# One VectorE sum of each seven-product unit moved behind three low parts

## The chip, the cores and the metric

The kernel runs on one core of one Trainium2 chip. The metric is the device time of one execution in microseconds (us). TensorE does the matmuls, VectorE (DVE in the profile) and ScalarE (ACT) prepare their operands, SyncE (SP) issues the transfers of the weights, and GpSimd (POOL) does a few small operations.

## The reference, cut to what matters

Two layers act on 256 positions of width 2048, in float32. Each layer is an input projection, two groups of heads (spatial gating and dilated attention), an output projection, and a feed-forward part:

```python
def reference(x, mix_norm, w_in, ..., w_gate, w_up, w_down):
    for l in range(DEPTH):
        ...
        x = x + mixed @ w_out[l]
        h = rms_norm(x, ffn_norm[l])
        x = x + (jax.nn.silu(h @ w_gate[l]) * (h @ w_up[l])) @ w_down[l]
    return x
```

The change lies in the feed-forward part: `w_gate` and `w_up` are 2048 x 5632, `w_down` is 5632 x 2048.

## The kernel before, in words

**Three matmuls for one.** To keep float32's precision, each operand is split in two parts. The high part (`wh`) is a copy of the tile rounded to fp32r, made on ScalarE; the low part (`wl`) is the tile minus its high part, made on VectorE (`split_w`, line 832). For each 128-row step, `mm3` (line 854) issues three matmuls: high x high, high x low and low x high, so the second matmul is the first that reads the weights' low part. Line 91 in the profile is the helper through which all instructions of ScalarE and VectorE go; they are told apart by their tiles.

**A unit.** In the feed-forward part, `unit` (line 892) multiplies a 2 x 2 arrangement of activation blocks by a 2 x 2 arrangement of weight blocks with seven products in place of eight. The weight blocks are raw tiles `b11`, `b12`, `b22` and `b21`, each loaded by one transfer (128 x 2048 elements where the unit has s = 4 steps, 128 x 1024 where s = 2). Sums of them are needed:

- `early` makes `e` = b12 - b11, then b12 = b22 - b12, before the unit's first item;
- `p1` splits b11, then makes b11 = b11 + b12;
- `p5` splits `e`, `p6` splits b11, `p2` makes b11 = b21 - b11 and splits b21, `p7` splits b12, `p3` splits b22, and `p4` splits b11.

So the seven products come in the order r1, r5, r6, r2, r7, r3, r4, here called the first to the seventh. The sum for the seventh product (b21 - b11) is made in `p2`, the preparation of the fourth. The first, fourth, ... products add into four banks of PSUM: the first and fourth into bank 1 (`C` in the profile), the second into Z (`CZ`), the third, fifth and seventh into X (`CX`), the sixth into Y (`CY`). Between products ScalarE copies banks: after the first product CX<-C, after the second `s`<-CZ, after the third CY<-CX, after the fifth `s`<-CX. After the sixth and the seventh, VectorE adds the saved copies to Z and Y.

Behind its seven products a unit has four plain items, which split one raw tile each and run 24 matmuls each.

**The order of the work.** The program is unrolled, and each engine runs its instructions in the order in which they are written out. All items, of all units, stand in one list. Before item n runs, `prep_more` (line 1065) writes out the preparations that fit a ring of six slots (two a full-size item): at full size that is the preparation of item n + 2. So the preparation of the sixth product (`p3`) is written behind the third product and its copy, and that of the seventh (`p4`) behind the fourth product. In the first unit of a layer's feed-forward part the sums begin five items ahead in place of one.

**The raw tiles.** `live` counts raw tiles in use; a preparation that is done with one lowers it, and `dma_more` issues the next load while it is under five. A layer has 17 units: chunks of four gate/up units and two down units twice, then a chunk of three gate/up units and two down units of s = 2. While a unit runs, jobs of others (the transposes `hTp` of the finished hidden block, and their copies `xg`) are written out between its matmuls.

The lines that the change touches are `p2` (929) and `p4` (942).

Of the kernel before, what the change touches and what calls it, by code (L numbers as in the profile page):

```python
# [12 lines left out]
ALU = mybir.AluOpType  # L13
# [129 lines left out]
def trunk_kernel(ctx: ExitStack, tc: tile.TileContext, aps: dict):  # L143
# [21 lines left out]
    def slot(shape, dtype, name):  # L165

        return gen.tile(list(shape), dtype, tag="g", name=name)
# [61 lines left out]
    def add(steps, limit=BACKLOG_NS):  # L229
        jobs.append(Job(steps, limit))  # L230
        jobs.sort(key=lambda job: -job.limit)

    def run_jobs(extra=0):
        for job in list(jobs):
            if job.t + MARGIN_NS <= q.pe and (job.when is None or job.when()):
                if q.backlog() <= job.limit + extra:
                    job.step()

    def drain(ready):
        stuck = 0  # L240
        while not ready():
            assert stuck < 2000, "operand is never made"
            stuck += 1
            q.pe += 100
            run_jobs(1000)
# [387 lines left out]
    def form(F, f, src):  # L633
        hi, lo = F.at(f)
        act.activation(out=hi, in_=src, func=ACTF.Copy)
        dve.tensor_tensor(out=lo, in0=src, in1=hi.bitcast(F32), op=ALU.subtract)
        F.ready.add(f)
# [169 lines left out]
    live = [0]  # L807
# [4 lines left out]
    def dma_one(r):  # L812
        n = sum(src.shape[1] for src in r.srcs)
        r.tile = slot([P, n, W], F32, "raw")
        k = 0
        for src in r.srcs:
            nc.sync.dma_start(out=r.tile[:, k:k + src.shape[1], :], in_=src)
            k += src.shape[1]
        live[0] += 1
# [6 lines left out]
    def need(r):  # L826
        while r.tile is None:
            dma_one(raws[n_raw[0]])
            n_raw[0] += 1
        return r.tile  # L830

    def split_w(src, parts=1):

        n = src.shape[1]
        if 2 * n <= 4:
            both = slot([P, 2, n, W], F32R, "w")
            wh, wl = both[:, 0], both[:, 1]
        else:
            wh, wl = slot([P, n, W], F32R, "wh"), slot([P, n, W], F32R, "wl")
        saved, q.chain = q.chain, q.pe  # L840
        for k in range(parts):
            sl = slice(k * n // parts, (k + 1) * n // parts)
            act.activation(out=wh[:, sl, :], in_=src[:, sl, :], func=ACTF.Copy)
            dve.tensor_tensor(
                out=wl[:, sl, :], in0=src[:, sl, :], in1=wh[:, sl, :].bitcast(F32), op=ALU.subtract)
        q.chain = saved
        return wh, wl

    def w_sum(out, in0, in1, op):
        saved, q.chain = q.chain, q.pe  # L850
        dve.tensor_tensor(out=out, in0=in0, in1=in1, op=op)
        q.chain = saved

    def mm3(out, x, wh, wl, start, stop):
        hi, lo = x
        for n, (a, b) in enumerate(((hi, wh), (hi, wl), (lo, wh))):
            nc.tensor.matmul(  # L857
                out=out, lhsT=a, rhs=b, start=start and n == 0, stop=stop and n == 2,
                skip_group_check=True)
# [32 lines left out]
    def unit(s, quarter, plains, form, done, lead=1):  # L892

        bank = {}
        b11, b12, b22, b21 = (Raw([quarter(*kn)], UNIT_RAW) for kn in ((0, 0), (0, 1), (1, 1), (1, 0)))
        raws.extend((b11, b12, b22, b21))
        U = {}

        def new_bank(name):
            drain(lambda: mm_lease.free)
            mm_lease.free.pop(0)
            bank[name] = mm_p.tile([P, W], F32, tag="mm", name="C" + name)

        def copy(out, in_):
            saved, q.chain = q.chain, q.pe
            act.activation(out=out, in_=in_, func=ACTF.Copy)
            q.chain = saved

        def early():
            x11, x12, x22 = need(b11), need(b12), need(b22)
            U["e"] = slot([P, s, W], F32, "e")
            live[0] += 1
            w_sum(U["e"], x12, x11, ALU.subtract)
            w_sum(x12, x22, x12, ALU.subtract)

        def p1(it, parts=1):
            it.w = split_w(b11.tile)
            w_sum(b11.tile, b12.tile, b11.tile, ALU.add)  # L920

        def p5(it, parts=1):
            it.w = split_w(U["e"])
            live[0] -= 1

        def p6(it, parts=1):
            it.w = split_w(b11.tile)

        def p2(it, parts=1):
            w_sum(b11.tile, need(b21), b11.tile, ALU.subtract)  # L930
            it.w = split_w(b21.tile)
            live[0] -= 1

        def p7(it, parts=1):
            it.w = split_w(b12.tile)
            live[0] -= 1

        def p3(it, parts=1):
            it.w = split_w(b22.tile)
            live[0] -= 1  # L940

        def p4(it, parts=1):
            it.w = split_w(b11.tile)
            live[0] -= 1

        def product(it, f, name, start):
            wh, wl = it.w
            for k in range(s):
                x = form(f, k)
                mm3(bank[name], x, wh[:, k, :], wl[:, k, :], start and k == 0, k == s - 1)  # L950
                q.pe += 3 * MM_NS
                run_jobs()

        def r1(it):
            new_bank("1")
            product(it, "11", "1", True)
            new_bank("X")
            copy(bank["X"], bank["1"])

        def r5(it):  # L960
            new_bank("Z")
            product(it, "S1", "Z", True)
            U["s5"], U["s3"] = (tmp.tile([P, W], F32, tag="u", name=n) for n in ("s5", "s3"))
            copy(U["s5"], bank["Z"])

        def r6(it):
            product(it, "S2", "X", False)
            new_bank("Y")
            copy(bank["Y"], bank["X"])

        def r2(it):
            product(it, "12", "1", False)

        def r7(it):
            product(it, "S3", "X", False)
            copy(U["s3"], bank["X"])

        def r3(it):
            product(it, "S4", "Y", False)
            w_sum(bank["Z"], bank["Z"], U["s3"], ALU.add)  # L980

        def r4(it):
            product(it, "22", "X", False)
            w_sum(bank["Y"], bank["Y"], U["s5"], ALU.add)

        for p, r in ((p1, r1), (p5, r5), (p6, r6), (p2, r2), (p7, r7), (p3, r3), (p4, r4)):
            items.append(Item(1 if s <= 2 else 2, UNIT_RING, p, r))
        early_at[len(items) - 7 - lead] = early

        names = {(0, 0): "1", (1, 0): "Y", (0, 1): "X", (1, 1): "Z"}  # L990
        for i, (n, srcs, ops) in enumerate(plains):
            r = Raw(srcs, UNIT_RAW)
            raws.append(r)

            def prep(it, parts=1, r=r):
                it.w = split_w(need(r))
                live[0] -= 1

            def run(it, i=i, n=n, ops=ops):
                wh, wl = it.w  # L1000
                for t in range(NT):
                    for k, op in enumerate(ops):
                        mm3(bank[names[n, t]], op(t), wh[:, k, :], wl[:, k, :], False, k == len(ops) - 1)
                        q.pe += 3 * MM_NS
                        run_jobs()
                    if i >= len(plains) - 2:
                        add(done(n, t, bank[names[n, t]]), FFN_LIMIT)
            items.append(Item(2, UNIT_RING, prep, run))
# [238 lines left out]
```

## Time and profile before

| | |
|---|---|
| median of 3 runs | 2277.02 us (2276.92 to 2278.56) |
| profiled execution | 2275.85 us, of which the span of the trace is 2273.7 us |
| TensorE busy | 2255.7 us (99%) |
| VectorE busy | 1828.6 us (80%) |
| ScalarE busy | 1322.1 us (58%) |
| moved by DMA | 440.34 MB, 194 GB/s |

Times in rows are in microseconds from the start of the span, and the name after an arrow in brackets is what ended the idle time before an instruction. `wl<-raw,wh` is an instruction that writes tile `wl` and reads tiles `raw` and `wh`. Rows of a timeline merge instructions that follow one another directly (x2 with one start and one duration). The end of a matmul is modelled.

### The profile page before, as it was taken

The numbers are of one execution on the slowest core, as the hardware profiler recorded it, in microseconds if no ns is written. First come the engines' busy times: TensorE is split into PE (matmuls) and PEld (weight loads), VectorE is DVE, ScalarE is ACT, GpSimd is POOL, SyncE is SP. The second block draws the span as 40 slices with busy tenths as digits, with TensorE's granted clock in tenths as the row PEclk, the third lists the DMA queues.
The fourth block names the chain that finished last, engine by engine and source line by source line (L and its number), as shares of the span: only waits on it lengthen the run. The fifth ranks groups of instructions, "written<-read, shape, count | busy, mean of one in ns | idle before, by whom it ended". The sixth has DMA issues, their size and how long they took to land.

```text
span 2273.7 us, 25953 instructions
## 1 busy us (share of the span) xinstructions
PE 2255.7 (99%) x10249; PEld 1863.7 (82%) x10249; DVE 1828.6 (80%) x1721; ACT 1322.1 (58%) x1590; POOL 59.2 (3%) x36
## 2 busy tenths in 40 slices
PE   9999999999999999999999999999999999999999
PEld 6888888888788888888888888888888888888887
DVE  6666766889999889988765666768998988989886
ACT  6555664565665665656655555646566546556563
POOL 0010000000000000000000001000000000000000
PEclk9999999999999999999999999999999999999999
DMA  9554545464564554745645444555546556447453
GB/s 351 192 185 151 182 152 215 165 227 154 186 246 180 209 209 149 259 185 192 227 167 196 163 167 167 185 185 196 192 167 215 211 194 223 176 168 275 167 204 111
DMA packets 66939, 440.34 MB, mean 194 GB/s; under 512 B 8065, under 2 KB 8577, under 8 KB 16769
## 3 DMA queue, kind: packets, MB, share of 16 engines
q1 hardware_dynamic: 66816, 438.69, 53.7%
q8 instruction: 80, 1.31, 0.2%
q14 instruction: 43, 0.34, 0.0%
HBM read 436.56 MB, written 2.10 MB: 193 GB/s over the span
## 4 chain that ended last, share of the span: by engine, by line
PE 82%; DVE 10%; issue 4%; ACT 2%; DMA 1%; SPq 0%; DVEq 0%; ACTq 0%
PE Z L857 33%; PE CX L857 16%; PE C L857 12%; PE CY L857 9%; PE CZ L857 8%; DVE wl L91 6%; DVE raw L91 1%; PE sc L473 1%; ACT wh L91 1%; DVE e L91 1%; PE hTp L260 1%; DMA gn<-in_k_norm 1%; PE qkp L260 1%; PE o L505 0%; DVE s L91 0%
## 5 line engine op out<-in xcount | busy, mean ns | idle before, releaser
L91 DVE TENSOR_TENSOR wl<-raw,wh 128x2048 fp32r<-128x2048 f32 x316 | 717.0, 2286 | 124.8 <-ACT wh L91 123.9
L91 ACT ACTIVATE wh<-raw 128x2048 fp32r<-128x2048 f32 x316 | 598.1, 1913 | 165.8 <-DVE wl L91 54.9
L857 PE MATMUL Z<-w,xT 128*128 128x512 f32 x2688 | 641.0, 395 | 3.6 <-ACT w L91 1.4
L857 PEld LDWEIGHTS Z<-w,xT 128*128 128x128 f32 x2688 | 499.0, 188 | 107.9 <-ACT w L91 2.3
L91 DVE TENSOR_TENSOR w<-raw,w 128x1024 fp32r<-128x1024 f32 (+1 forms) x313 | 376.5, 1216 | 216.5 <-ACT w L91 212.3
L91 ACT ACTIVATE w<-raw 128x1024 fp32r<-128x1024 f32 (+1 forms) x313 | 315.6, 1050 | 21.9 <-DMA raw<-in_w_in 9.8
L91 DVE TENSOR_TENSOR raw<-raw 128x2048 f32<-128x2048 f32 (+1 forms) x102 | 220.6, 2163 | 2.5
L857 PE MATMUL CX<-wh,fF 128*128 128x512 f32 x528 | 175.5, 391 | 0.0
L857 PE MATMUL C<-wh,fF 128*128 128x512 f32 x352 | 117.2, 391 | 0.0
L857 PEld LDWEIGHTS CX<-wh,fF 128*128 128x128 f32 x528 | 99.1, 188 | 20.4
L857 PE MATMUL C<-wh,fT 128*128 128x512 f32 x352 | 115.5, 389 | 0.0
L857 PE MATMUL CY<-wh,fT 128*128 128x512 f32 x352 | 115.5, 389 | 0.0
L857 PE MATMUL CZ<-wh,fT 128*128 128x512 f32 x352 | 115.5, 389 | 0.0
L857 PE MATMUL CX<-wh,fT 128*128 128x512 f32 x352 | 115.5, 389 | 0.0
L857 PE MATMUL CX<-wl,fF 128*128 128x512 f32 x264 | 102.7, 389 | 0.0
L857 PE MATMUL Z<-w,bT 128*128 128x512 f32 x384 | 89.9, 391 | 0.0
L91 ACT ACTIVATE CX<-C 128x512 f32<-128x512 f32 x34 | 19.8, 582 | 120.3 <-PE C L857 120.3
L857 PE MATMUL Z<-w,aT 128*128 128x512 f32 x384 | 88.8, 390 | 0.0
L857 PEld LDWEIGHTS Z<-w,aT 128*128 128x128 f32 x384 | 71.8, 188 | 14.8
L857 PEld LDWEIGHTS Z<-w,bT 128*128 128x128 f32 x384 | 71.8, 188 | 14.7
L857 PE MATMUL CY<-wh,fF 128*128 128x512 f32 x240 | 79.9, 391 | 0.0
L857 PEld LDWEIGHTS C<-wh,fT 128*128 128x128 f32 x352 | 66.1, 188 | 13.7
(191 smaller groups left out, 3444.9 us busy)
## 6 DMA issues: line engine op xcount, KB each, us to landing
raw<-in_w_in SPq DMA_DIRECT2D x109, 1024.0 KB, 4.8
raw<-in_w_gate SPq DMA_DIRECT2D x88, 1024.0 KB, 4.9
raw<-in_w_up SPq DMA_DIRECT2D x88, 1024.0 KB, 4.9
raw<-in_w_down SPq DMA_DIRECT2D x72, 1024.0 KB, 4.8
raw<-in_w_out SPq DMA_DIRECT2D x32, 1024.0 KB, 4.8
raw<-in_w_down SPq DMA_DIRECT2D x32, 512.0 KB, 5.0
raw<-in_w_in SPq DMA_DIRECT2D x5, 512.0 KB, 8.0
xstage<-in_xT SPq DMA_DIRECT2D x8, 256.0 KB, 7.5
```

What stands on the lines that cost most here:

```text
L91: return f(**kw)
L260: nc.tensor.transpose(out=tp[:, i, t * P:(t + 1) * P], in_=src_of(t)[:, (c0 + i) * P:(c0 + i + 1) * P], identity=ident)
L473: nc.tensor.matmul(out=sc[:, g, :n], lhsT=L.kv[pair, g][:, h, t * P:(t + 1) * P], rhs=kT[:, h, :n], start=True, stop=True)
L857: nc.tensor.matmul(out=out, lhsT=a, rhs=b, start=start and n == 0, stop=stop and n == 2, skip_group_check=True)
```

## The change

The sum b11 = b21 - b11 goes from the front of `p2` to the front of `p4`. `p2` is left with the split of b21. Raw tile b21 is given back in `p4` in place of `p2`, so `live` falls by two there. The number of instructions is the same.

```diff
         def p2(it, parts=1):
-            w_sum(b11.tile, need(b21), b11.tile, ALU.subtract)
-            it.w = split_w(b21.tile)
-            live[0] -= 1
+            it.w = split_w(need(b21))
...
         def p4(it, parts=1):
+            w_sum(b11.tile, b21.tile, b11.tile, ALU.subtract)
             it.w = split_w(b11.tile)
-            live[0] -= 1
+            live[0] -= 2
```

On VectorE a unit's order of these was: sum, fourth low part, fifth, sixth, seventh. It becomes: fourth low part, fifth, sixth, sum, seventh. On ScalarE the order of the copies is as before.

## Rows read from the trace of the kernel before

**Rows 1.** The page's first part: engine, busy us, share of the span, instructions.

```profile
PE 2255.7 (99%) x10249; PEld 1863.7 (82%) x10249; DVE 1828.6 (80%) x1721; ACT 1322.1 (58%) x1590; POOL 59.2 (3%) x36
```

**Rows 2.** The tile `e` on VectorE, one instruction a unit: durations ns, first and last start.

```profile
L91 DVE TENSOR_TENSOR e<-raw x34: 1214/2283/2291, 421.7 to 2225.2; 128x2048 f32<-128x2048 f32 x30, 128x1024 f32<-128x1024 f32 x4
```

**Rows 3.** Timeline of VectorE in a gate/up unit: start, duration, instruction, count, [idle before].

```profile
1036.43 2.28 DVE L91 TENSOR_TENSOR raw<-raw 128x2048 f32<-128x2048 f32 x1
...
1041.11 2.29 DVE L91 TENSOR_TENSOR wl<-raw,wh 128x2048 fp32r<-128x2048 f32 x1 [0.20 <-ACT wh L91]
1043.83 4.49 DVE L91 TENSOR_TENSOR wl<-raw,wh 128x2048 fp32r<-128x2048 f32 x2 [0.43 <-ACT wh L91]
```

**Rows 4.** Timeline of ScalarE in the same unit.

```profile
1041.39 0.58 ACT L91 ACTIVATE CY<-CX 128x512 f32<-128x512 f32 x1 [0.31 <-PE CX L857]
1041.89 3.71 ACT L91 ACTIVATE wh<-raw 128x2048 fp32r<-128x2048 f32 x2
1045.50 0.58 ACT L91 ACTIVATE xg<-hTp 128x512 f32<-128x512 f32 x1
1047.76 0.60 ACT L91 ACTIVATE s<-CX 128x512 f32<-128x512 f32 x1 [1.68 <-PE CX L857]
1048.25 1.91 ACT L91 ACTIVATE wh<-raw 128x2048 fp32r<-128x2048 f32 x1
```

**Rows 5.** Timeline of TensorE in the same unit: transposes, seventh product, first plain item.

```profile
1044.60 1.04 PE L260 MATMUL hTp<-ident,s 128*128 128x128 f32 x8
...
1050.51 0.39 PE L857 MATMUL CX<-wl,fF 128*128 128x512 f32 x1
...
1053.23 0.39 PE L857 MATMUL C<-wl,fT 128*128 128x512 f32 x1
```

**Rows 6.** Timeline of VectorE in the fourth unit of layer 0.

```profile
576.63 2.28 DVE L91 TENSOR_TENSOR raw<-raw 128x2048 f32<-128x2048 f32 x1
578.83 8.89 DVE L91 TENSOR_TENSOR wl<-raw,wh 128x2048 fp32r<-128x2048 f32 x4
```

**Rows 7.** Timeline of TensorE in that unit, at the fourth product.

```profile
581.17 0.50 PE L857 MATMUL C<-wl,fF 128*128 128x512 f32 x1 [1.21 <-DVE wl L91]
```

**Rows 8.** The list of waits: engine, line, what for; us in total, times, longest.

```profile
PEld C L857 <- DVE wl L91: 15.9, 17, 1.7
...
ACT w L91 <- DMA raw<-in_w_in: 9.8, 5, 3.7
...
PE C L857 <- DVE wl L91: 8.5, 8, 1.3
```

**Rows 9.** The tile `hTp` on TensorE: durations ns, first and last start.

```profile
L260 PE MATMUL hTp<-ident,s x176: 270/273/273, 497.7 to 2220.7; 128*128 128x128 f32 x176
```

**Rows 10.** Timeline of VectorE in the first gate/up unit of the second chunk.

```profile
709.44 4.49 DVE L91 TENSOR_TENSOR wl<-raw,wh 128x2048 fp32r<-128x2048 f32 x2 [0.43 <-ACT wh L91]
```

**Rows 11.** Timeline of TensorE in that unit, at the seventh product.

```profile
715.19 0.39 PE L857 MATMUL CX<-wl,fF 128*128 128x512 f32 x1
```

**Rows 12.** Timeline of VectorE in the first down unit of the first chunk.

```profile
620.81 6.88 DVE L91 TENSOR_TENSOR wl<-raw,wh 128x2048 fp32r<-128x2048 f32 x3
```

**Rows 13.** Timeline of TensorE in that unit, at the seventh product.

```profile
632.37 0.39 PE L857 MATMUL CX<-wl,hF 128*128 128x512 f32 x1
```

**Rows 14.** Timeline of VectorE in a down unit of half-size tiles: the seventh low part.

```profile
1077.96 1.23 DVE L91 TENSOR_TENSOR w<-raw,w 128x1024 fp32r<-128x1024 f32 x1 [1.07 <-ACT w L91]
```

**Rows 15.** Timeline of TensorE in that unit: the seventh product's first matmuls.

```profile
1083.42 1.30 PE L857 MATMUL CX<-w,hF 128*128 128x512 f32 x5
```

**Rows 16.** Timeline of VectorE in the first unit of layer 0: the seventh low part.

```profile
442.89 2.28 DVE L91 TENSOR_TENSOR wl<-raw,wh 128x2048 fp32r<-128x2048 f32 x1
```

**Rows 17.** Timeline of TensorE in that unit, at the seventh product.

```profile
463.22 0.39 PE L857 MATMUL CX<-wl,fF 128*128 128x512 f32 x1
```

**Rows 18.** The view of cores: span and mean granted clock.

```profile
core 0: 2273.7 us, clock 1.000
```

**Rows 19.** Timeline of TensorE at the start: the warm-up matmuls.

```profile
1.25 4.02 PE L1133 MATMUL warm<-junk 128*128 128x512 bf16 x9 [1.25 <-DVE junk L1128]
```

## The prediction

> **What bounds the kernel now.** I read the page's busy table first. TensorE is busy for 99% of the span [rows 1], so a microsecond in which it cannot issue is a microsecond of the time, and no other engine's saving counts unless it ends such a gap. Next I read how many units there are: 34, of which 30 have tiles of 128x2048 and 4 have tiles of 128x1024 [rows 2]. The edit lies in each of them and nowhere else. Then I read one unit in order of time on VectorE, on ScalarE and on TensorE, a gate/up unit in the middle of layer 0 [rows 3 to 5], and looked in each product for the matmul that reads the low part. That is the second matmul of the product, since the first needs the high part alone.
>
> What the reader is to see there is a chain of copies, not a full engine. The low part of the sixth product starts at 1043.83, after VectorE stood idle for 0.43 us waiting for its high part [rows 3]. That high part is on ScalarE behind the copy CY<-CX, which starts at 1041.39, when the third product has ended on TensorE, 0.31 us after ScalarE came free [rows 4]. So the low parts of the fifth and sixth products are tied to TensorE's own progress. The fifth low part, at 1041.11, stood 0.20 us for its high part in the same way [rows 3]. Their times are not set by how much work VectorE has, and work taken from VectorE ahead of them does not make them earlier. The seventh low part follows the sixth at once: two in 4.49 us, the second from 1046.03 to 1048.32 [rows 3]. TensorE first reads it at 1050.51 [rows 5], 2.19 us later. This lead is what the edit draws on.
>
> **Where there is something to gain.** In some units TensorE does wait for the low part of the fourth product. In one of them the sum runs from 576.63 and the low part from 578.83 to 581.12 [rows 6], and TensorE's second matmul of that product starts at 581.17 after an idle time of 1.21 us [rows 7]. The waits of this kind add up to 8.5 us on the matmuls and 15.9 us on the weight loads over the whole trace [rows 8]. An idle time in this list begins at the modelled end of a matmul (0.39 us), while matmuls start 0.227 us apart (twelve in 2.72 us from 1050.51 to 1053.23 [rows 5]), so each is some 0.16 us longer than listed. With the smaller waits that only the weight-load row counts I take 13 us for all of them, between the bounds 8.5 and 15.9.
>
> **The change, part by part.** No instruction is added or removed: 34 sums move, each past three low parts on VectorE.
>
> Moved away, ahead of the fourth low part: a sum of 2.2 us (576.63 to the next start at 578.83 [rows 6]). The fourth low part can start up to 2.2 us sooner, and every wait listed above was at most 1.7 us long [rows 8], so I take all of them as ended: minus 13 us. In the other units the fourth low part is held by its high part, and the gain there is nothing.
>
> Moved in, behind the sixth low part: the seventh's high part reads what the sum writes, so ScalarE cannot begin it before the sum ends, and VectorE, which keeps its order, stands idle behind the sum until the high part is there. Before, the sum was long done by then: it started at 1036.43 and took 2.28 us [rows 3], and the seventh high part ran right behind the sixth (two from 1041.89 in 3.71 us [rows 4]), under the sixth low part. From the end of the sixth low part at 1046.12 (1043.83 + 2.29 [rows 3]) I now count the sum to 1048.32 (in the place of the old low part), a hand-over of 0.04 us (as from 581.12 to 581.17 [rows 6, 7]), the high part of 1.91 us [rows 4] to 1050.27, 0.03 us, and the low part of 2.29 us to 1052.59. TensorE reads it at 1052.64 instead of 1050.51: 2.13 us lost in this unit. The seventh low part is 4.27 us later than before; the lead of 2.19 covers half.
>
> How much lead there is in the other units depends on what TensorE does between the end of the third product and the seventh. In this unit the eight transposes at 1044.60 [rows 5] lengthen it by 0.9 us. Eight of the seventeen units of a layer look like this, counted by where the sets of eight of the 176 transposes [rows 9] fall. Where no transposes fall there the lead is shorter. In another unit [rows 10, 11] the sixth low part starts at 709.44 and the second matmul of the seventh product at 715.19. The steps above took 8.81 us from the start of the sixth low part to that matmul (1043.83 to 1052.64), which gives 718.25 here: 3.06 us. I count four units of a layer so: the first gate/up unit of a chunk and the second down unit. In the first down unit the seventh high part waited for other things already: low parts four to six ran from 620.81 to 627.69 [rows 12], so after the change the seventh would be ready at about 634.2, against 632.37 [rows 13]: 1.83 us. Two units of a layer.
>
> Six units lose nothing. In the four with half-size tiles the seventh low part ends at 1079.19 [rows 14] and is read 0.23 us behind 1083.42 [rows 15], a lead of 4.46 us, and all three steps there are half as long (1.23 us for a low part), which makes the shift about 2.4 us. In the first unit of a layer the low part that ends at 445.17 is for the product whose matmul starts at 463.22 [rows 16, 17].
>
> Sum over two layers: 16 x 2.13 + 8 x 3.06 + 4 x 1.83 = 34.1 + 24.5 + 7.3 = 65.9 us. A matmul that restarts the stream is longer, 0.50 us [rows 7] against 0.39 [rows 5]: 28 x 0.11 = 3.1 us.
>
> What is queued behind: on ScalarE, behind the waiting high part, stand the copy of transposes xg<-hTp, the copy s<-CX and the high part of the first plain item [rows 4]. The copy s<-CX must be read before the seventh product may write its bank again; it would end at about 1051.3, before the seventh product can go on at 1052.64, so it costs nothing. The first plain high part would then run from 1051.3 to 1053.2 and its low part to 1055.5, where TensorE wants it at 1052.64 + 11 x 0.227 + 0.23 = 1055.37: a loss of 0.1 to 0.2 us where such transposes are copied, 16 x 0.1 = 1.6 us. After that the four plain items give VectorE 21.8 us of matmuls for some 9 us of low parts, and it recovers: I find the next unit's first sum at most 1 us later with respect to TensorE, and the next fourth low part has been relieved of 2.2 us.
>
> DMAs: the second raw tile b21 is given back three items later, so the raw tiles of the second to fourth plain items are issued one item (2.72 us) later each on SP's queue. The only wait of ScalarE for a weight tile in the list of waits is in the input projection, 9.8 us [rows 8], none in a unit, so I cost this at nothing. If that cover were gone in a few units, it would be at most 2.72 us in each.
>
> Total: 65.9 + 3.1 + 1.6 - 13 = 57.6, say 58 us. The profiled execution took 2275.85 us (span 2273.7 and 2.2 us around it); with 58 it is 2333.9. The median of the runs, 2277.02, is 1.2 us above it, so I forecast 2335 us.
>
> **The rivals.** *Faster.* The seventh low part is still in time and only the gain is left: 2277 - 13 = 2264 us. This takes one mechanism, that the sixth low part, freed of the sum, ends at least 2.1 us sooner with respect to TensorE, and it decides from a lead of 4.27 us. For it: VectorE has the room. Against it: the idle 0.43 us ahead of the sixth low part and the copy that its high part waits for [rows 3, 4]. Chance 0.04.
>
> *No change.* No engine gets more or less work, and the gain of 13 us would pay for a loss of 0.46 us a unit in 28 units: 2277 us. The smallest loss that I find is 1.83 us. Chance 0.03. The Trainium skill (Perfetto Trace Analysis, Identifying Performance Opportunities) has it that improving a kernel generally means improving its most-contended engine; read alone this would give this rival, since no engine's busy time changes, and the trace does not bear it out, as the wait on a part of VectorE's work that only comes late shows [rows 7].
>
> *The clock falls.* The 28 new gaps of 2 to 3 us could bring TensorE's clock from its higher level (2.4 GHz) to its lower (1.2 GHz). The granted clock is 1.000 over the whole span [rows 18], and after the gap at 581.17 the matmuls went on at the higher level. No gap in this trace after the start is longer. At the lower level nine warm-up matmuls took 4.02 us, 0.42 us apart [rows 19]. If the twelve matmuls after each gap ran so, it would cost 28 x 12 x 0.2 = 67 us more: 2402 us. Chance 0.05. The Trainium skill (TensorE: Matmul & The Clock Gate, Part 1) says that the array is throttled by default and activity releases it, which speaks for this rival; nothing in this trace shows it for gaps of 2 to 3 us.
>
> *The lateness carries over.* If VectorE did not recover within the plain items, the next fourth product would wait as before and the 13 us would not come: 2348 us. Chance 0.10. This lies within my range.
>
> **How the numbers follow.** My forecast has 0.78. Its bounds: at the low end every one of 28 units loses the smallest 1.83 us and the gain is 15.9, 51 - 16 = 35, or 2312 us; at the high end all lose 3.06, the restarts cost 3.1 and the gain is only 8.5, 85.7 + 3.1 - 8.5 = 80.3, or 2358 us. The lateness rival is inside, the other three, 0.12, are outside. About 0.2% (4.5 us) is what a measurement can tell from no change: faster by more 0.04, within 0.04, slower 0.92.
>
> **What would show it.** In the profile after: in each full-size unit an idle time of VectorE of about 1.95 us between the sum and the seventh low part, and one of ScalarE ahead of the seventh high part released by that sum; 28 waits of TensorE of 1.7 to 3 us on bank CX released by wl, where now there is none; no waits on bank C for the fourth low part; VectorE, ScalarE and TensorE busy as before; the granted clock at 1.000. The prediction is wrong if the sixth low part ends earlier with respect to TensorE than rows 3 to 5 have it, or if the bank CX waits are few.

## The result, and the profile after

The change makes the kernel slower: 2370.88 us, median of 2363.95, 2372.68, 2373.15 and 2369.07, against 2277.36 us for the kernel before on the same chip. The ratio is 1.0413, 95% interval 1.0401 to 1.0425, or 94 us. The forecast was 2335 us with a range up to 2358: the direction is right, the time lies 13 us outside. The profiled execution is the shortest of the four, with a span of 2361.7 us.

The page's busy table of the changed kernel, beside [rows 1]:

```profile
PE 2286.1 (97%) x10249; PEld 1872.8 (79%) x10249; DVE 1833.9 (78%) x1721; ACT 1319.6 (56%) x1590; POOL 58.8 (2%) x36
```

The counts are as before, and VectorE and ScalarE are as busy as before. TensorE is 30 us busier with the same matmuls, so some matmuls took longer; the other 58 us of span are idle time. The view of cores, where [rows 18] has a clock of 1.000:

```profile
core 0: 2361.7 us, clock 0.991
```

The other three executions have 0.987, 0.987 and 0.988. Next the list of waits, beside [rows 8]; each line is engine, tile, what for, us in total, times, longest:

```profile
DVE wl L91 <- ACT wh L91: 202.7, 165, 4.4
ACT wh L91 <- DVE raw L91: 163.6, 41, 4.9
...
PE CX L857 <- ACT s L91: 33.4, 31, 2.6
...
PE CX L857 <- DVE wl L91: 31.1, 30, 1.4
```

The wait of bank C for wl, 8.5 us in [rows 8], is gone. In its place stand two waits on bank CX in each full-size unit, one for the copy `s` and one for `wl`. The timeline of the gate/up unit of [rows 3 to 5] (it is layer 0's last gate/up unit), after, on VectorE, ScalarE and TensorE in turn:

```profile
1082.40 2.29 DVE L91 TENSOR_TENSOR wl<-raw,wh 128x2048 fp32r<-128x2048 f32 x1 [0.43 <-ACT wh L91]
1084.61 2.29 DVE L91 TENSOR_TENSOR raw<-raw 128x2048 f32<-128x2048 f32 x1
1088.94 2.29 DVE L91 TENSOR_TENSOR wl<-raw,wh 128x2048 fp32r<-128x2048 f32 x1 [2.04 <-ACT wh L91]
...
1086.99 1.92 ACT L91 ACTIVATE wh<-raw 128x2048 fp32r<-128x2048 f32 x1 [4.62 <-DVE raw L91]
1088.82 0.57 ACT L91 ACTIVATE xg<-hTp 128x512 f32<-128x512 f32 x1
1089.29 0.59 ACT L91 ACTIVATE s<-CX 128x512 f32<-128x512 f32 x1
...
1071.61 0.39 PE L857 MATMUL C<-wh,fF 128*128 128x512 f32 x1
...
1089.93 0.49 PE L857 MATMUL CX<-wh,fF 128*128 128x512 f32 x1 [0.91 <-ACT s L91]
1091.29 0.50 PE L857 MATMUL CX<-wl,fF 128*128 128x512 f32 x1 [0.86 <-DVE wl L91]
```

Here is the line of three steps that was forecast. The sixth low part still waits 0.43 us for its high part; behind it come the sum, ScalarE's high part 0.09 us after the sum's end, and the low part, with VectorE idle for 2.04 us between. The copy `s` stands behind the waiting high part, so the seventh product's first matmul waits as well, and one delay shows as two idle times. The unit's first matmul, at 1071.61 here, was this row of the kernel before:

```profile
1033.04 0.39 PE L857 MATMUL C<-wh,fF 128*128 128x512 f32 x1
```

The second matmul of the seventh product came 17.47 us behind it before ([rows 5]) and comes 19.68 us behind it now: 2.21 us, against 2.13 forecast.

Summed by product (the time from a product's first matmul to the next one's, less 0.227 us a matmul and 0.11 us a transpose, over all units) the fourth product's loss fell from 14.7 to 1.9 us. The seventh's rose from nothing to 39 us ahead of its first matmul and 57 us within it, of which 11 us are matmuls at 0.427 us.

### The profile page after: what moved, and what is told of

It is laid out like the page before. It is cut to its first block, busy times and chain, and to the rows that moved or that the text cites. A ratio compares the mean times of both kernels' runs of the same rounds, so it can differ in the third digit from the quotient of the medians.

```text
span 2361.7 us, 25916 instructions
## 1 busy us (share of the span) xinstructions
PE 2286.1 (97%) x10249; PEld 1872.8 (79%) x10249; DVE 1833.9 (78%) x1721; ACT 1319.6 (56%) x1590; POOL 58.8 (2%) x36
## 4 chain that ended last, share of the span: by engine, by line
PE 80%; DVE 10%; ACT 6%; issue 3%; DMA 1%; SPq 0%; ACTq 0%; DVEq 0%
PE Z L857 32%; PE CX L857 15%; PE C L857 11%; PE CZ L857 10%; PE CY L857 7%; DVE wl L91 5%; ACT wh L91 5%; DVE raw L91 3%; PE sc L473 1%; DMA gn<-in_k_norm 1%; ACT CY L91 1%; PE qkp L260 1%; DVE w L91 1%; PE o L505 0%; DMA xstage<-in_xT 0%
## 5 line engine op out<-in xcount | busy, mean ns | idle before, releaser
L857 PE MATMUL CX<-wh,fF 128*128 128x512 f32 x528 | 184.2, 408 | 22.8 <-ACT s L91 22.8
L857 PE MATMUL CX<-wl,fF 128*128 128x512 f32 x264 | 108.9, 413 | 22.2 <-DVE wl L91 22.2
L857 PEld LDWEIGHTS Z<-w,bT 128*128 128x128 f32 x384 | 71.8, 188 | 14.7
L857 PEld LDWEIGHTS CX<-wl,fF 128*128 128x128 f32 x264 | 51.6, 195 | 39.3 <-DVE wl L91 29.2
```

The costliest lines, as they stand in the source:

```text
L857: nc.tensor.matmul(out=out, lhsT=a, rhs=b, start=start and n == 0, stop=stop and n == 2, skip_group_check=True)
```

## The experiments

Each was timed against the kernel before on the same chip: 2275.46 us beside e1 to e4, 2275.61 us beside e5 to e7, 2275.57 us beside e8 and e9, and 2275.36 us beside e10. Unless said otherwise, a diff is against the kernel before.

**The late raw tile by itself (e1).** The sum stays where it was; only the return of b21 moves to `p4`.

```diff
 def p2:
-            live[0] -= 1
...
 def p4:
-            live[0] -= 1
+            live[0] -= 2
```

> The sum stays ahead of the fourth low part; only raw tile b21 is counted as given back three items later, so the raw tiles of the plain items are asked for later. Theory (the exposed high part and low part of the seventh product are the loss): 2277 us, within 3 us of before, no waits of TensorE on bank CX. Rival (the late raw tiles are part of the loss): 2285 us or more, with waits of ScalarE for weight tiles inside the units.

Measured: 2275.31 us, ratio 1.0004 (0.9995 to 1.0013). The later transfers cost nothing, as the forecast had it.

**The sum one low part earlier than in the change (e2)**, ahead of the sixth product's split:

```diff
 def p2:
-            w_sum(b11.tile, need(b21), b11.tile, ALU.subtract)
-            it.w = split_w(b21.tile)
-            live[0] -= 1
+            it.w = split_w(need(b21))
...
 def p3:
+            w_sum(b11.tile, b21.tile, b11.tile, ALU.subtract)
             it.w = split_w(b22.tile)
-            live[0] -= 1
+            live[0] -= 2
```

> The sum is made one item sooner than in the changed kernel: ahead of the sixth low part, still behind the fourth and fifth. Theory: the seventh high part now runs under the sixth low part again, so its 1.91 us and the idle VectorE are gone. The sixth low part comes 1.75 us later against a lead of 1.6 us (with transposes) or 0.74 us (without): some 0.1 us lost in 16 units and 1 us in 8 to 12, and the 13 us of the fourth product are gained: 2270 to 2280 us, and the granted clock is 1.000. Rival (a sum that stands behind low parts costs by its place on VectorE): 2320 us or more.

Measured: 2280.77 us, ratio 1.0025 (1.0016 to 1.0035), 0.8 us above the expected range. The sum stands only one low part earlier than in the changed kernel, and the loss is 5 us in place of 94. VectorE's timeline in the same gate/up unit:

```profile
1042.38 2.29 DVE L91 TENSOR_TENSOR wl<-raw,wh 128x2048 fp32r<-128x2048 f32 x1 [0.36 <-ACT wh L91]
1044.58 2.29 DVE L91 TENSOR_TENSOR raw<-raw 128x2048 f32<-128x2048 f32 x1
1046.79 4.49 DVE L91 TENSOR_TENSOR wl<-raw,wh 128x2048 fp32r<-128x2048 f32 x2
```

From the list of waits of that run:

```profile
PEld CY L857 <- DVE wl L91: 23.1, 30, 1.3
PE CY L857 <- DVE wl L91: 11.5, 14, 0.8
```

The two low parts run on without an idle time, since the seventh high part has its operand while VectorE is at the sixth low part. What is left is 2.2 us of VectorE's time against the sixth product's lead: by product the sixth loses 18.8 us more than before and the fourth wins 13.8. So the large loss is ScalarE's 1.91 us and the second hand-over, which nothing covers once the sum is next to its own low part.

**The sum one low part later than before (e6)**, between the fourth and the fifth:

```diff
 def p2:
-            w_sum(b11.tile, need(b21), b11.tile, ALU.subtract)
-            it.w = split_w(b21.tile)
+            it.w = split_w(need(b21))
+            w_sum(b11.tile, b21.tile, b11.tile, ALU.subtract)
```

> The kernel before, with the sum b21 - b11 written one low part later: behind the split of b21, so between the fourth and the fifth low parts. The seventh high part then has its operand early, as before. Theory (what a low part loses is the time by which the sum's end comes behind that of the wait that held the low part already): the fourth product gains the same 13 us as in the changed kernel, the seventh and sixth lose nothing or little, as both are held by copies; the fifth low part, which stood only 0.20 us for its high part, comes up to 2.1 us later. TensorE's fifth product waits for it by about 1.1 us in the units whose low parts ran one behind another: 28 x 1.1 - 13 = +18, so 2290 to 2300 us, with no wait of the seventh product. Rival (any place behind the fourth low part that leaves the seventh high part its operand is free): 2264 us. If the seventh product still waits by 2 us a unit, the theory is wrong.

Measured: 2285.34 us, ratio 1.0041 (1.0026 to 1.0056), 5 us better than the expected range. The fifth product loses 25.4 us in all: about 1.2 us in 18 units, as expected, but only 0.3 us in the other twelve, for most of which I had counted 1.1. No wait on `s` or on the seventh low part appears. The rival, that any early place is free, falls.

**The changed kernel's place, with the three steps in halves (e3).** Diff against the changed kernel:

```diff
 def p4:
-            w_sum(b11.tile, b21.tile, b11.tile, ALU.subtract)
-            it.w = split_w(b11.tile)
+            h = s // 2
+            for sl in (slice(0, h), slice(h, s)):
+                w_sum(b11.tile[:, sl, :], b21.tile[:, sl, :], b11.tile[:, sl, :], ALU.subtract)
+            it.w = split_w(b11.tile, 2)
```

> The changed kernel's place, but the sum and the seventh product's two copies are made in two halves each: sum, sum, then low parts. Theory: the chain from the end of the sixth low part to the first half of the seventh low part shortens from 6.5 to about 3.7 us, so TensorE's wait before the seventh product falls from 2.2 to 3.3 us to between 0 and 0.5 us, and the gain of 13 us at the fourth product shows: 2262 to 2272 us, granted clock 1.000. Rival (the place behind the three low parts is the loss whatever the chain): 2340 us or more.

Measured: 2360.15 us, ratio 1.0376 (1.0362 to 1.0390): a miss by 90 us. The seventh product's waits did shrink, from 96 to 24 us by product. But the program's own costs, by which jobs are fitted between matmuls, count the added instructions, and the written order changed: in four down units the next unit's preparations came ahead of a copy that TensorE needed, and each of these units loses 9.0 to 9.9 us behind its seventh product. Two half-size units lose 6.7 us each in their first four products, and most other units 1.1 to 1.2 us behind the seventh. So this run does not settle what the halves are worth; the next one does. TensorE's timeline in one of them:

```profile
656.81 0.50 PE L857 MATMUL C<-wh,hT 128*128 128x512 f32 x1 [0.91 <-ACT hT L91]
663.22 1.22 PE L857 MATMUL C<-wh,hT 128*128 128x512 f32 x2 [5.68 <-DVE hT L91]
```

**The same halves, in full-size units alone, with the program's costs kept (e7).** The sum, high part and low part of `p4` are issued in two halves each, and the costs of the unsplit ones are booked (core of the diff against the changed kernel):

```diff
 def p4, where s == 4:
+            q.spend("dve", dve_cost("", s * W, {}))
...
+            for sl in (slice(0, h), slice(h, s)):
+                nc.vector.tensor_tensor(
+                    out=x[:, sl, :], in0=y[:, sl, :], in1=x[:, sl, :], op=ALU.subtract)
+            for sl in (slice(0, h), slice(h, s)):
+                nc.scalar.activation(out=wh[:, sl, :], in_=x[:, sl, :], func=ACTF.Copy)
+                nc.vector.tensor_tensor(
+                    out=wl[:, sl, :], in0=x[:, sl, :], in1=wh[:, sl, :].bitcast(F32),
+                    op=ALU.subtract)
```

> The changed kernel, with sum, high part and low part of the seventh product's operand made in two halves of 128x1024 each, in the full-size units alone, and the program's own costs for the written order left as in the changed kernel. Theory (the seventh product waits for the line of three steps, and halving the steps overlaps them): its wait falls from 2.1 us to 0 to 0.7 us, the first plain item is up to 1 us late in each unit, the order of the first down units stays as in the changed kernel, and TensorE's clock stays up for lack of gaps of 2 us: 2285 to 2310 us. Rival (the loss is not in the overlap of the three steps but in the lateness of everything behind them): 2340 us or more, as the changed kernel without its clock loss.

Measured: 2318.75 us, ratio 1.0190 (1.0173 to 1.0207): 9 us above the expected range, well under the rival's. The order losses are gone and the clock is 0.998 to 1.000. VectorE's timeline in the unit of [rows 10]:

```profile
720.21 2.35 DVE L956 TENSOR_TENSOR raw<-raw 128x1024 f32<-128x1024 f32 x2
722.56 2.37 DVE L960 TENSOR_TENSOR wl<-raw,wh 128x1024 fp32r<-128x1024 f32 x2
725.98 2.29 DVE L91 TENSOR_TENSOR wl<-raw,wh 128x2048 fp32r<-128x2048 f32 x1 [1.06 <-ACT wh L91]
```

From the list of waits:

```profile
PE C L857 <- DVE wl L91: 25.2, 29, 0.9
...
PE CX L857 <- ACT s L91: 8.9, 11, 1.8
```

VectorE no longer waits between sum and low part. The lateness moved on: ScalarE comes later to the first plain item's high part, and that item's second matmul waits in 29 units, 25.2 us as listed and 30 us with the 0.16 us that each start hides. I had counted at most 1 us a unit and forgotten the first units, where the seventh product still loses 3.9 and 2.3 us (in one of them 1.4 us of it are seven matmuls 0.43 us apart, the rate of the lower clock level that the next experiment shows).

**Filler matmuls in the gap (e4).** The changed kernel, with nine matmuls of a constant bf16 tile into an unused bank ahead of each full-size unit's seventh product. Diff against the changed kernel:

```diff
 def r4:
...
+            for _ in range(9 if s == 4 else 0):
+                nc.tensor.matmul(
+                    out=fill[:, :W], lhsT=filler[:, :P], rhs=filler, start=True, stop=True)
             product(it, "22", "X", False)
```

> The changed kernel with nine matmuls of a constant tile (2.04 us at the higher clock level) put ahead of each full-size unit's seventh product, where TensorE waits; they add nothing to the result. Theory (a part of the loss is the lower clock after the waits): the granted clock is back at 1.000, the matmuls at 0.427 us behind the waits are gone, and the time is 2352 to 2360 us, 10 to 18 us below the changed kernel, though it has more matmuls. Rival (the waits are the whole loss): 2368 to 2374 us. If the nine do not fit the gap, up to 61 us more.

Measured: 2348.0 us, ratio 1.0318 (1.0302 to 1.0333). More work makes it 22 us faster than the changed kernel, (1.0413 - 1.0318) x 2276, 4 us more than expected. The line of three steps is as late as before: the second matmul of the seventh product comes 19.69 us behind its unit's first in the unit shown here (19.70 without filler), and 21.30 us in the first unit of layer 0 (the same without). The clock is what changed. TensorE's timeline in one unit of the changed kernel, at the seventh product:

```profile
687.67 0.39 PE L857 MATMUL CY<-wh,fF 128*128 128x512 f32 x1
689.43 0.50 PE L857 MATMUL CX<-wh,hF 128*128 128x512 f32 x1 [1.37 <-ACT s L91]
691.27 0.79 PE L857 MATMUL CX<-wl,hF 128*128 128x512 f32 x1 [1.34 <-DVE wl L91]
691.86 1.05 PE L857 MATMUL CX<-wh,hF 128*128 128x512 f32 x2
...
694.93 0.40 PE L857 MATMUL CX<-wl,hF 128*128 128x512 f32 x1
695.16 0.39 PE L857 MATMUL CX<-wh,hF 128*128 128x512 f32 x1
```

And the view of stretches there (stretch, length, busy us of PE, PEld, DVE, ACT and POOL, TensorE's granted clock, DMA share, GB/s):

```profile
686.00:689.50 3.50, 2.13 (x11) 1.43 (x9) 1.44 (x2) 2.52 (x3) 0.00 (x0) 1.00 1.01 421
689.50:693.00 3.50, 2.16 (x5) 1.55 (x6) 3.50 (x2) 3.48 (x2) 0.00 (x0) 0.73 1.00 421
693.00:696.00 3.00, 3.00 (x11) 2.35 (x11) 3.00 (x3) 0.64 (x1) 0.00 (x0) 0.75 1.02 415
```

After the second of the two waits, matmuls start 0.43 us apart, the rate of the lower level (1.2 GHz), and from about 694.7 again 0.23 us apart. With filler, the timeline at the same product (the trace has a record of eight of the nine):

```profile
684.75 2.12 PE L985 MATMUL fill<-filler 128*128 128x512 bf16 x8
686.52 0.58 PE L858 MATMUL CX<-wh,hF 128*128 128x512 f32 x1
688.13 0.50 PE L858 MATMUL CX<-wl,hF 128*128 128x512 f32 x1 [1.02 <-DVE wl L91]
```

The same view of stretches from there on, through the first plain item:

```profile
688.00:692.00 4.00, 3.87 (x17) 3.22 (x18) 4.00 (x4) 3.11 (x3) 0.00 (x0) 1.00 1.01 424
692.00:696.00 4.00, 4.00 (x20) 3.30 (x19) 4.00 (x4) 2.45 (x2) 0.00 (x0) 1.00 0.93 387
```

The Trainium skill (TensorE: Matmul & The Clock Gate, Part 1) says that the array is throttled by default and activity releases it; this pair of runs agrees, with a clock of 1.00 with filler and 0.73 without in the same product.

**Filler, and the six units of the forecast left alone (e10).** As the last one, but with the sum in its old place, and no filler, in the first unit of each layer and the four half-size units (`p4` likewise):

```diff
 def p2:
+            if s < 4 or lead > 1:
+                w_sum(b11.tile, need(b21), b11.tile, ALU.subtract)
+                it.w = split_w(b21.tile)
+                live[0] -= 1
+                return
```

> The changed kernel with the filler matmuls ahead of the seventh product, but with the sum left in its old place in the six units that the forecast's sum left out (the first unit of each layer and the four of half size, without filler there). Theory (the forecast's sum for 28 units is right, and what it missed is the two first units, the half-size units and the clock): 2348.0 less 8.5 for the first units and 2 to 3 for the half-size ones gives 2336 to 2338 us, beside the 2335 of the forecast, with the clock at 1.000 and no long wait in a first unit. Rival (the forecast's terms for the 28 units are off too, and the agreement of single units is chance): outside 2330 to 2342 us.

Measured: 2337.54 us, ratio 1.0271 (1.0254 to 1.0288), within the expected 2336 to 2338. This is the kernel that the forecast's sum describes, 28 units with a full clock, and it stands 62 us above before, where the sum said 58. The six units together cost 10.5 us.

**The sum on GpSimd (e5)**, in its old place in the order:

```diff
 def p2:
-            w_sum(b11.tile, need(b21), b11.tile, ALU.subtract)
...
+            pool.tensor_tensor(out=b11.tile, in0=need(b21), in1=b11.tile, op=ALU.subtract)
...
```

> The kernel before, with one edit: the sum b21 - b11 is written out where it was, in the preparation of the fourth product, but on GpSimd; VectorE has one instruction less in each unit. Theory (the loss of the changed kernel is a three-step line sum, high part, low part that begins only behind the sixth low part; its gain of 13 us is VectorE freed of 2.2 us ahead of the fourth low part): the gain stays, and the seventh product loses nothing if GpSimd ends the sum before ScalarE comes to the seventh high part, some 7 to 8 us after the sum's start (from 1036.4 to about 1043.8 in the gate/up unit read). Then the time is 2262 to 2266 us. Rival: GpSimd needs longer than that for 128x2048 elements, or slows VectorE's low parts beside it; then the seventh product waits for GpSimd, and the time is above 2277 us, by 0.3 us per 10 us for each 1 % that VectorE's instructions get longer where they are late, and by the whole lateness of the sum in 30 units.

Measured: 2315.26 us, ratio 1.0174 (1.0159 to 1.0189): a miss. The rival's range holds, and it named slower low parts beside GpSimd, but it had the seventh product wait, and it is the fourth that does. The timeline in a down unit, of GpSimd, VectorE and TensorE in turn, at the fourth product:

```profile
669.22 4.62 POOL L91 TENSOR_TENSOR raw<-raw 128x2048 f32<-128x2048 f32 x1 [41.68 <-DMA raw<-in_w_down]
...
670.11 5.87 DVE L91 TENSOR_TENSOR wl<-raw,wh 128x2048 fp32r<-128x2048 f32 x1 [0.37 <-ACT wh L91]
...
676.04 0.50 PE L857 MATMUL C<-wl,hF 128*128 128x512 f32 x1 [2.74 <-DVE wl L91]
```

The group of all low parts of 128x2048 (busy us, mean ns, idle before):

```profile
L91 DVE TENSOR_TENSOR wl<-raw,wh 128x2048 fp32r<-128x2048 f32 x316 | 772.9, 2464 | 172.9 <-ACT wh L91 168.7 <-DMA raw<-in_w_down 2.3
```

The low part takes 5.87 us in place of 2.29 [rows 3]. It began 0.89 us into GpSimd's sum, which ended at 673.84, and ended 2.14 us behind that, at 675.98, just ahead of TensorE's matmul: as if it had begun when GpSimd was done. So it is wherever a low part starts beside a full-size GpSimd sum: each ends 2.1 to 2.2 us behind the sum's end. Over the program low parts of this form take 772.9 us, against 717.0 in the kernel before, and by product the fourth loses 54.4 us where it lost 14.7: the 39.7 us between the two medians. Some 6 us of it are the clock's: in five of the 16 units where it waits 2.2 to 3.4 us from start to start, matmuls 0.43 us apart follow, 30 in all, and the clock is 0.996. The Trainium skill (SBUF — State Buffer, SBUF: two separate sides) has it that a GpSimd instruction and a VectorE one with two inputs in SBUF share a port pair, which the one that starts first holds to its end while the other is blocked; the 5.87 us agree.

**The sum behind the fifth low part in 16 units alone (e8)**, those in which the fourth product waits: `p2` and `p3` as in the second experiment, switched by a flag that is set for the third and fourth gate/up unit of a chunk of four and the full-size down units.

```diff
 def p3:
+            if late:
+                w_sum(b11.tile, b21.tile, b11.tile, ALU.subtract)
+                live[0] -= 1
             it.w = split_w(b22.tile)
```

> The kernel before, with the sum b21 - b11 moved behind the fifth low part (ahead of the sixth product's split) in 16 units alone: those four of each of the first two chunks of a layer in which the fourth product waits by 0.31 to 1.55 us in the kernel before. The other 18 units stay as before. Theory (gain at the fourth product and loss at the sixth are separate and add up unit by unit): by the units' periods in the run with that move everywhere, against before, 42.15 becomes 41.97, 43.24 becomes 42.85, 42.01 becomes 41.94 and 42.02 becomes 41.93: 0.73 us for four units, 2.9 us for 16, so a ratio of about 0.9987, 2.9 us below before. Rival (each unit hands its lateness to the next, so that the choice of units doesn't matter): no change, or slower by up to 5 us.

Measured: 2273.47 us, ratio 0.9991 (0.9981 to 1.0000), 2.1 us below before where 2.9 was expected: not to be told from no change. By product the fourth wins 13.8 us and the sixth loses 11.0, as the units did in the run with all of them. Lateness does not pile up from unit to unit.

**The sum in four quarters (e9)**, one ahead of each of the fourth to seventh low parts, in 28 units, with the seventh high and low parts in halves and the program's costs kept:

```diff
 def p2, p7, p3, p4, where s == 4 and lead == 1:
+            quarter_sum(k)          # k = 0, 1, 2, 3
...
+        def quarter_sum(k):
+            nc.vector.tensor_tensor(
+                out=b11.tile[:, k, :], in0=b21.tile[:, k, :], in1=b11.tile[:, k, :], op=ALU.subtract)
```

> The kernel before, with the sum b21 - b11 cut in four quarters of 128x512 in 28 units (not in the first unit of a layer and not in the four of half size): one quarter ahead of the fourth, the fifth, the sixth and the seventh low part each; the seventh high and low parts are made in two halves. The program's own costs for the written order are kept. Theory (each low part may come later by its own lead and by the idle time of 0.2 to 0.43 us that stands ahead of it, and not more; only what exceeds that is lost): a quarter is some 0.6 us. The fourth product is relieved of 1.6 us and gains its 13 us; the fifth and sixth low parts get 0.2 and 0.4 us later against leads of about 0.7, which costs nothing; the seventh is ready some 1.2 us later than before, against leads of 1.2 and 2.2, which costs 0 to 0.3 us; the first plain item loses nothing to 0.3 us. 13 less 28 x (0 to 0.5): 2263 to 2276 us, with a best guess of 2268. Rival (TensorE's stream follows the sum of VectorE's instructions, wherever they are cut): no faster than before.

Measured: 2272.05 us, ratio 0.9982 (0.9973 to 0.9991), in the expected range though 4 us above its best guess: 3.5 us under before by medians, small but with an interval below 1. VectorE's timeline in the unit of [rows 3]:

```profile
1040.12 0.68 DVE L943 TENSOR_TENSOR raw<-raw 128x512 f32<-128x512 f32 x1
1040.73 2.29 DVE L91 TENSOR_TENSOR wl<-raw,wh 128x2048 fp32r<-128x2048 f32 x1
1042.93 0.69 DVE L943 TENSOR_TENSOR raw<-raw 128x512 f32<-128x512 f32 x1
1043.53 2.44 DVE L972 TENSOR_TENSOR wl<-raw,wh 128x1024 fp32r<-128x1024 f32 x2
```

The one longer wait for a low part that the list of waits has left:

```profile
PEld C L857 <- DVE wl L91: 9.9, 26, 0.8
```

A quarter costs 0.6 us, of which the idle time ahead of a low part (0.20 and 0.43 us in [rows 3]) takes a part and the lead over TensorE the rest. The losses of the seven products together fall from 16.7 to 4.6 us. Most of these 12 us, some 8, are lost again behind the seventh product, at the first plain item, where the weight load for bank C waits in 26 places, 9.9 us as listed.

## Why the prediction was wrong

**The main step that failed is the clock.** The sum and its range kept it at 1.000, and the rival in which it falls had a chance of 0.05 and was all or nothing: twelve slow matmuls after each of 28 gaps, 67 us. The clock fell after some of the waits, and that cost 22 us. In the profiled execution eight full-size units are longer than in the filler run, together 13.3 us: both first units, five of the eight with the longest waits (about 3.2 us), and one of the other twenty. Another 2.1 us lie ahead of the first unit, where the change has no part. The other executions, at a lower clock, are 5 to 9 us longer still. With the clock held up the same program takes 2348.0 us, inside the range. That filler cures it is shown; why one wait drops the clock and its like does not is open. What I lacked was a partial case: "No gap in this trace after the start is longer" says nothing against the clock falling, and the gaps that I forecast were up to twice the longest that the trace had shown to be harmless (idle times of 1.21 to 1.25 us, four of them).

**"Six units lose nothing" failed too: 10.5 us.** In the first unit of a layer I took the low part of [rows 16] for the seventh's. Its sums begin early, but the ring of slots lets only three preparations run ahead, and the row is the third product's. The seventh's is the second of these two in the kernel before:

```profile
458.02 4.49 DVE L91 TENSOR_TENSOR wl<-raw,wh 128x2048 fp32r<-128x2048 f32 x2 [1.32 <-ACT wh L91]
```

It ends at 462.51 and is read at 463.22 [rows 17], a lead of 0.71 us and not of 18. The forecast's shift of 4.27 us would have given a loss of 3.56 us here; measured, the second matmul of the seventh product comes 21.30 us behind the unit's first for 17.68, or 3.62 us. The timeline of VectorE and TensorE there, in the changed kernel:

```profile
461.97 2.28 DVE L91 TENSOR_TENSOR raw<-raw 128x2048 f32<-128x2048 f32 x1
466.24 2.29 DVE L91 TENSOR_TENSOR wl<-raw,wh 128x2048 fp32r<-128x2048 f32 x1 [1.98 <-ACT wh L91]
...
467.47 0.50 PE L857 MATMUL CX<-wh,fF 128*128 128x512 f32 x1 [2.58 <-ACT s L91]
468.58 0.50 PE L857 MATMUL CX<-wl,fF 128*128 128x512 f32 x1 [0.61 <-DVE wl L91]
```

The seventh low part ends at 468.53 and is read 0.05 us later. With the clock full such a unit takes 46.26 us in place of 42.0: 8.5 us for the two. The four half-size units make the other 2.0. Their seventh low part has its lead as forecast, but the line of three steps holds up what stands behind it. In the first of them VectorE's read of a bank (`s<-CZ,r,s`) starts 4.82 us behind the unit's first matmul for 4.34 before, the copy CY<-CX, which follows that read before and after, at 5.66 us for 5.18, and the fifth product loses 0.5 us. In the second the transposes stand in another place, and its part is not taken further apart here.

The parts of the difference, from the runs: 62 us for the 28 units where the sum said 58, 10.5 for the six where it said nothing, 22 for the clock where it said nothing: 94.5, against 94 measured. Each part is the difference of one run from the next, so that they add up is no test by itself. Without the clock's part the time would have been inside the range; without that of the six units alone it would not.

**What held.** The path of the loss, a line of sum, high part and low part exposed behind the sixth low part, and its size: 2.21 us for 2.13 in the gate/up unit, 3.07 for 3.06 in the unit of [rows 10, 11] (16.55 us from its first matmul to the second of the seventh product before, 19.62 now), 2.2 for 1.83 in the first down unit (17.76 and 19.68, and 0.3 lost at its fourth product before). Over the 28 units, with the fourth product's gain set aside, the seventh product's second matmul comes 69.0 us later in all, where the sum had 65.9. The gain at the fourth product: 12.8 us for 13. The raw tiles: nothing. The restarts are as forecast, 0.50 us. The plain items' 1.6 us fell elsewhere: none of them waits by more than 0.2 us, and 0.4 us stand in the first two products of the fourth gate/up unit of four chunks. "The copy `s<-CX` costs nothing" holds: the low part is later still, in the first units too, where the copy's wait of 2.58 us is listed ahead of the low part's 0.61 but the low part ends last (468.53, read at 468.58).

**The other rivals.** A free gain (2264 us) and no change fall with the result. Lateness that carries over falls with the loss at the fourth product, which is gone.

## What to carry to other kernels

When an instruction is moved behind others on an in-order engine, count its successors on the other engines and back: one VectorE sum of 2.2 us next to its own low part exposed ScalarE's 1.9 us and a second low part, while the same sum one low part earlier cost 5 us in place of 94. A step with no slack of its own is best cut up and laid into idle times that are there already. Before a forecast puts new gaps of several microseconds into a dense matmul stream, give a partial fall of the clock a chance and a price of its own.

## What the runs showed of the hardware

Two waits with a single matmul between them (687.67 to 689.43 to 691.27, 1.76 and 1.84 us from start to start) were followed by the lower level of TensorE's clock, here for some eight matmuls, and by no fall in most units of the same run. In the GpSimd run a single wait of 2.2 to 3.4 us from start to start was followed by it in 5 of 16 units. Nine matmuls of filler ahead of the seventh product, which are work for nothing, bought 22 us.

A GpSimd sum of 128x2048 took 4.62 us where VectorE's takes 2.28, and held VectorE's low part back to its end: 5.87 us for 2.29.

Cutting VectorE's f32 instructions is cheap: 128x1024 twice took 2.35 us for 2.28, and 128x512 0.60 us from start to start, four for 2.4.
